# When results are stored: earlier and then later stores, buffers held one slot longer, and two sets of carries on SyncE's queue

## The chip, the core and the metric

The kernel runs on one core of a Trainium2 chip. PE is TensorE (matrix products), DVE is VectorE, ACT is ScalarE, POOL is GpSimd, and SP is SyncE, which here only issues DMA transfers. The metric is the device time of one execution in microseconds (us).

## The reference

For each of 16 batches and 256 channels, a recurrence runs over 2048 time steps. It is the weighted average of the values v with weights exp(k) that fade with time by exp(-w); `pp` only keeps the exponents from overflowing:

```python
for t in range(seq_len):
    ww = u + kk
    qq = np.maximum(pp, ww)
    e1, e2 = np.exp(pp - qq), np.exp(ww - qq)
    output[b, t, :] = (e1 * aa + e2 * vv) / (e1 * bb + e2 + 1e-08)
    ww = pp - w + kk
    qq = np.maximum(ww, kk)
    e1, e2 = np.exp(ww - qq), np.exp(kk - qq)
    aa = e1 * aa + e2 * vv
    bb = e1 * bb + e2
    pp = qq
```

Numerator and denominator are the same sum with v and without it. k and v are 33.6 MB each, the output 33.6 MB, all float32.

## The kernel before

**Tiles.** Time is cut into 16 stages of 128 steps (numbered c), the batches into 4 groups of 4. A tile n = 4c + p is stage c of group p: 128 steps on the partitions, 4 batches x 256 channels along the free side, 0.5 MB. There are 64 tiles. Each needs a load of k, a load of v and a store, each a single DMA of 0.5 MB issued by SP.

**A tile's way.** DVE rounds k into `km` (L193) and casts v to bf16 (L227), PE forms the exponents (`logs`, L203 and L209), ACT takes their exponentials (`exps`, L222), DVE multiplies these by v (`times_v`, L233). Ten slots later (LAG = 10) PE sums the denominator with a triangular matrix (`den`, L360), ACT takes its logarithm into an output buffer (`den_log`, L365) and turns it into the reciprocal there (`den_exp`, L368), PE sums the numerator (`num`, L377), DVE multiplies both (`mult`, L381), and SP stores the buffer (`store`, L385).

**Carries.** What goes from stage to stage is computed per stage in small steps: `sums`, `copy_sums`, `turn`, `state_logs`, `state_frames`, `state_scan`, `state_offsets`, `state_weights`, `state_chain`, `turn_back`, `inject`. The last one casts the carries (L345) and writes them with four small DMAs (L350) over two rows of the exponentials of the stage's own four tiles, where `den` and `num` of these tiles read them. The first two of the four go where `den` reads. POOL issues these DMAs for stages 0 to 14, SP for stage 15. The carries of stage 14 are wanted by tiles 56 to 59, those of stage 15 by tiles 60 to 63.

**Order.** The order is written out by hand: every instruction stands in its engine's queue in the order of the program. The main loop counts slots n = 0 to 63; in slot n the exponentials of tile n are taken, q = n - 10 is the tile whose denominator is formed, qp = n - 11 the one whose product is formed. The dictionary `later` places the steps for the carries in later slots. After slot 63 a tail does the last ten tiles.

**Buffers.** 19 buffers of 0.5 MB serve loads and outputs alike. `take` hands out the one whose slot number is lowest. A loaded buffer is free again in the slot in which it is cast. An output buffer is free STORED slots after the slot of its store (L386). `loads` (L79) moves a buffer from the loads' list to the outputs' when fewer than three of these will be free; then it issues loads while they are under nine slots ahead and two buffers are free. These slot numbers decide only who gets which buffer: that the store has landed is waited for on the chip, by the logarithm that writes the buffer.

**SP's queue.** SP works in program order. A load waits for the cast that frees its buffer, a store for its product. Which stores a slot issues is said in L485:

```python
while stored < (qp - 2 - max(0, n - 20) // 12 if loaded < NP else qp):
    store(stored, n)
```

So stores are two slots late at first, three from slot 32, four from slot 44, five from slot 56, and all at once when the last load has been issued. The tail stores what is left, then tile 53 (`store(q, q + LAG)`, L533), then has the last carries issued (L539), then stores the other tiles as they come. The last tile goes out in four quarters, by SP and ACT (L558).

Of the kernel before, what the change touches and what calls it, by code (L numbers as in the profile page):

```python
# [15 lines left out]
def kernel(  # L16
# [10 lines left out]
    PE, DVE, SC, POOL, SP = nc.tensor, nc.vector, nc.scalar, nc.gpsimd, nc.sync  # L27
# [4 lines left out]
    NST = T // TC  # L32
    D = 2 * Dm
    NP = 4 * NST
    RING = 12
    BUFS, OUTS = 19, 8
    STORED = 4
    LAG = 10
    RS = 2.0 ** -20
    CAP = 54.0  # L40
# [11 lines left out]
    def rows_of(x, n):  # L52
        c, p = divmod(n, 4)
        return x[4 * p:4 * p + 4, c * TC:(c + 1) * TC, :].rearrange("n t d -> t n d")
# [4 lines left out]
    free = [(0, x) for x in bufs[OUTS:]]  # L59
    free_out = [(0, x) for x in bufs[:OUTS]]  # L60

    def take(slot, of):
        j = min(range(len(of)), key=lambda j: of[j][0])
        assert of[j][0] <= slot
        return of.pop(j)[1]

    def load_k(n, slot=0):
        kr_of[n] = take(slot, free)
        K(SP.dma_start(out=kr_of[n], in_=rows_of(k, n)))

    def load_v(n, slot=0):
        vr_of[n] = take(slot, free)
        K(SP.dma_start(out=vr_of[n], in_=rows_of(v, n)))
# [3 lines left out]
    loaded = 5  # L77

    def loads(slot):  # L79
        nonlocal loaded  # L80
        if slot + 2 >= LAG and sum(x <= slot + 2 for x, _ in free_out) < 3:
            free_out.append((slot + 2, take(slot, free)))
        while loaded < NP and loaded - slot < 9 and sum(x <= slot for x, _ in free) >= 2:
            load_v(loaded, slot)
            loaded += 1
            if loaded < NP:
                load_k(loaded, slot)
# [102 lines left out]
    def round_k(n, slot=0):  # L190
        km = consts.tile([128, 4, Dm], F32R, tag=f"km{n % 2}", name="km") if n < 2 else KM[n - 2]
        kr = kr_of.pop(n)
        K(DVE.tensor_copy(km, kr))  # L193
        free.append((slot, kr))
        KM[n] = km

    def logs(n):
        km = KM[n].rearrange("p (i n) d -> p i (n d)", i=2)

        def rows(q):  # L200
            for i in range(2):
                g = 32 * (2 * q + i)
                K(PE.matmul(half(n, q)[:, i, :], CO[g:g + 32, :],  # L203
                            WU[g:g + 32, :].unsqueeze(1).broadcast_to([32, 2, Dm]), start=True, stop=False,
                            tile_position=(g, 0), skip_group_check=True))

        def steps(q):
            for i in range(2):
                K(PE.matmul(half(n, q)[:, i, :], (NLE, NLZ)[q], km[:, i, :], start=False, stop=True,  # L209
                            skip_group_check=True))  # L210

        rows(0)
        rows(1)
        steps(0)
        steps(1)

    def exps(n):
        if n < TURNS:
            for q in range(2):
                K(SC.activation(ez(n)[:, q], half(n, q), ACT.Exp))  # L220
        else:
            K(SC.activation(ez(n)[:, 0:2], PS[:, 0:4, :].rearrange("p (q i) x -> p q i x", q=2), ACT.Exp))  # L222

    def cast_v(n, slot=0):
        vb = vbpool.tile([128, 4, Dm], BF16, tag="vb", name="vb")
        vr = vr_of.pop(n)
        K(DVE.tensor_copy(vb, vr))  # L227
        free.append((slot, vr))
        VB[n] = vb

    def times_v(n):
        vb = VB.pop(n).rearrange("p (i n) d -> p i (n d)", i=2)
        K(DVE.tensor_mul(ez(n)[:, 2:4], ez(n)[:, 0:2], vb.unsqueeze(1).broadcast_to([128, 2, 2, D])))  # L233
# [109 lines left out]
    def inject(c, queue=POOL):  # L343
        cb = small.tile([128, 128], BF16, tag="cb", name="cb")
        K(DVE.tensor_copy(cb, st.pop((c, "CT"))))  # L345
        r0 = 4 * c % RING
        for q in range(2):
            for h in range(2):
                r, x = HS * h + HS - 1, 32 * (2 * q + h)
                K(queue.dma_start(  # L350
                    out=EZR[r:r + 1, 2 * q, r0:r0 + 4, :, :].rearrange("o p i (b x) -> o (p i b) x", b=4),
                    in_=cb[x:x + 32, :]))
# [4 lines left out]
    def den(n, bank=DENB):  # L357
        for m, q in (("L", 0), ("Id", 1)):
            for i in range(2):
                K(PE.matmul(bank[:, i, :], mats[m], ez(n)[:, q, i, :], start=q == 0, stop=q == 1,  # L360
                            skip_group_check=True))
# [13 lines left out]
    def num(n, bank, i):  # L375
        for m, q in (("LN", 2), ("IdN", 3)):
            K(PE.matmul(bank, mats[m], ez(n)[:, q, i, :], start=q == 2, stop=q == 3, skip_group_check=True))  # L377

    def mult(n, bank, i):
        rd = RD[n]  # L380
        K(DVE.tensor_mul(rd[:, i, :], bank, rd[:, i, :]))  # L381

    def store(n, slot):
        rd = RD.pop(n).rearrange("p i (n d) -> p (i n) d", n=2)
        K(SP.dma_start(out=rows_of(out, n), in_=rd))  # L385
        free_out.append((slot + STORED, rd))  # L386

    later = {}
    for c in range(NST):
        s = 4 * c + 3  # L390
        plan = [(s + 1, "act" if s + 1 < LAG else "recip", copy_sums), (s + 1, "pe", turn),
                (s + 2, "act", state_logs), (s + 2, "mid", state_frames), (s + 2, "scan", state_scan), (s + 2, "scan", state_offsets),
                (s + 3, "recip", state_weights), (s + 3, "chain", state_chain),
                (s + 4, "nums", turn_back), (s + 4, "mid", inject), (s + 4, "mid", state_next)]
        if c == 0:
            plan = [(s + 1, "act", copy_sums), (s + 1, "pe", turn), (s + 1, "pe", state_logs),
                    (s + 1, "round", state_frames), (s + 1, "round", state_scan), (s + 1, "round", state_offsets),
                    (s + 2, "act", state_weights), (s + 2, "round", state_chain),
                    (s + 3, "pe", turn_back), (s + 3, "round", inject), (s + 3, "round", state_next)]
        if c == 1:  # L400
            plan = [(s + 1, "act", copy_sums), (s + 1, "pe", turn), (s + 2, "act", state_logs),
                    (s + 2, "round", state_frames), (s + 2, "round", state_scan), (s + 2, "round", state_offsets),
                    (s + 3, "recip", state_weights), (s + 3, "early", state_chain)] + plan[8:]
        if c == NST - 1:
            plan = []
        for slot, where, f in plan:
            later.setdefault((slot, where), []).append((f, c))

    def small_work(n, where):
        for f, c in later.pop((n, where), []):  # L410
            f(c)
# [35 lines left out]
    stored = 0  # L447

    def inverses(n):
        q, qp = n - LAG, n - LAG - 1  # L450
        if qp >= 0:
            num(qp, NUMB, 1)

        sums(n - 1)
        if n + 1 < NP:
            recip(q, lambda: small_work(n, "recip"))

    for n in range(LAG, NP):

        q, qp = n - LAG, n - LAG - 1  # L460
        if qp >= 0:
            num(qp, NUMB, 0)
        den(q)
        small_work(n, "nums")
        exps(n)
        small_work(n, "act")
        if qp >= 0:
            mult(qp, NUMB, 0)
        small_work(n, "mid")
        if n == LAG:  # L470

            inverses(n)
            small_work(n, "early")
        if n + 2 < NP:
            round_k(n + 2, n)

        if n % 4 in (3, 0):
            cast_v(n, n)
        if n + 1 == NP:
            times_v(n)  # L480
        elif n % 4 < 2:
            cast_v(n + 1, n)
        loads(n)

        while stored < (qp - 2 - max(0, n - 20) // 12 if loaded < NP else qp):  # L485
            store(stored, n)
            stored += 1
        if n > LAG:
            inverses(n)
        if qp >= 0:  # L490
            mult(qp, NUMB, 1)
        small_work(n, "scan")
        if n + 1 < NP:
            times_v(n)
            small_work(n, "chain")
            logs(n + 1)
        small_work(n, "pe")
# [4 lines left out]
    q, c = NP - LAG - 1, NST - 1  # L502
# [4 lines left out]
    def outputs(n):  # L507
        for i in range(2):
            mult(n, nbank(n, i), i)
        store(n, n + LAG)  # L510
# [19 lines left out]
    state_offsets(c)  # L530
    state_weights(c)
    mult(q, nbank(q, 1), 1)
    store(q, q + LAG)  # L533
    state_chain(c)
    den(q + 3, dbank(q + 3))
    for i in range(2):
        tile_num(q + 1, i)
    turn_back(c)
    inject(c, SP)  # L539
    outputs(q + 1)  # L540
    for n in range(q + 2, NP):
        if n + 1 < NP:
# [8 lines left out]
    n, p = NP - 1, (NP - 1) % 4  # L551
# [38 lines left out]
```

## Time and profile before

| | |
|---|---|
| median of 3 runs | 286.34 us (285.8 to 286.8) |
| profiled execution | 285.23 us, its span 283.5 us |
| DVE busy | 261.1 us (92%) |
| PE busy | 256.2 us (90%) |
| ACT busy | 253.6 us (89%) |
| POOL busy | 106.0 us (37%) |
| moved by DMA | 101.54 MB, mean 358 GB/s |
| TensorE clock granted | 0.994 |

The span runs from the first to the last instruction of the profiled execution; 1.7 us of its time lie around it. Issuing a DMA doesn't count as busy. In lines of a timeline the columns are start (us), duration (us), engine, line and operation, written and read tiles, count, and in brackets the engine's idle time before it with what ended it. A busy share is an average over the whole span; a wait counts where something stands behind it.

### The profile page before, as it was taken

The page shows a single profiled execution, that of the slowest core. Times are in us where ns is not written, and L with a number is a line of the kernel's source. Part 1 is how long each engine was busy: PE and PEld are TensorE (multiplying, and loading weights), DVE is VectorE, ACT ScalarE, POOL GpSimd, SP SyncE. Part 2 cuts the span into 40 slices and gives each one's busy share as a digit, 9 for nine tenths or more (in the row PEclk, how much of TensorE's full clock was granted, in tenths as well). Part 3 has the DMA queues.
Part 4 walks back from the last instruction along what each step waited for, and adds up shares of the span by engine and source line. Part 5 has one row for each costly group of instructions (what it writes and reads, how often), then busy time and mean ns, then how long its engine had stood idle before and what let it go on. Part 6 is the DMA issues. An engine that isn't in the chain of part 4 may idle for free.

```text
span 283.5 us, 5049 instructions
## 1 busy us (share of the span) xinstructions
PE 256.2 (90%) x1662; PEld 119.5 (42%) x1694; DVE 261.1 (92%) x465; ACT 253.6 (89%) x252; POOL 106.0 (37%) x206
## 2 busy tenths in 40 slices
PE   6997896999999999999999999899999999997990
PEld 2444442544454444544454444444444344433430
DVE  4699989999999999999999999999999999987863
ACT  2576678999999999999999999899999999997991
POOL 7000424263445444253445445143546546242000
PEclk9999999999999999999999999999999999999997
DMA  6999999999999999999999999999999999999597
GB/s 225 349 348 350 348 331 350 333 348 352 384 375 382 384 381 385 383 382 382 384 377 384 375 384 377 378 376 369 382 379 384 383 384 378 380 384 334 167 340 252
DMA packets 103586, 101.54 MB, mean 358 GB/s; under 512 B 4284, under 2 KB 103560, under 8 KB 103560
## 3 DMA queue, kind: packets, MB, share of 16 engines
q1 hardware_dynamic: 101336, 100.45, 103.9%
q0 software_dynamic: 1920, 0.50, 0.8%
q8 instruction: 13, 0.21, 0.3%
q10 hardware_dynamic: 304, 0.27, 0.3%
q14 instruction: 13, 0.11, 0.1%
HBM read 67.12 MB, written 33.55 MB: 355 GB/s over the span
## 4 chain that ended last, share of the span: by engine, by line
DVE 35%; PE 27%; DMA 16%; ACT 9%; issue 9%; DVEq 1%; POOL 0%; ACTq 0%; POOLq 0%
DVE EZR L233 14%; DVE buf L381 11%; PE PS L377 9%; PE PS L209 9%; DMA buf<-in_k_dram 7%; DMA out_dram<-buf 6%; PE PS L257 3%; PE PS L203 3%; ACT EZR L222 3%; ACT buf L365 3%; DVE vb L227 3%; DVE km L193 3%; PE PS L360 2%; ACT buf L368 2%; DMA EZR<-cb 2%
## 5 line engine op out<-in xcount | busy, mean ns | idle before, releaser
L222 ACT ACTIVATE EZR<-PS 128x2048 bf16<-128x2048 f32 x54 | 101.2, 1874 | 3.3 <-PE PS L209 2.6
L381 DVE TENSOR_TENSOR buf<-PS,buf 128x512 f32<-128x512 f32 x128 | 87.6, 692 | 6.3 <-ACT buf L368 4.2
L233 DVE TENSOR_TENSOR EZR<-EZR,vb 128x2048 bf16<-128x2048 bf16 x64 | 78.3, 1224 | 3.1 <-ACT EZR L220 2.5
L365 ACT ACTIVATE buf<-PS 128x1024 f32<-128x1024 f32 x64 | 65.8, 1028 | 3.4 <-DMA out_dram<-buf 1.6
L368 ACT ACTIVATE buf<-buf 128x1024 f32<-128x1024 f32 (+1 forms) x65 | 67.9, 1049 | 0.9
L377 PE MATMUL PS<-EZR,LN 128*128 128x512 bf16 x128 | 48.8, 381 | 10.3 <-DVE buf L381 6.7
L350 POOL DMA_DIRECT2D EZR<-cb x60 | 36.7, 617 | 52.0 <-DVE cb L345 44.6
L209 PE MATMUL PS<-km,NLE 128*128 128x512 f32 x128 | 47.6, 454 | 1.8 <-DVE km L193 1.8
L193 DVE CAST km<-buf 128x1024 fp32r<-128x1024 f32 x64 | 44.2, 691 | 1.3 <-DMA buf<-in_k_dram 1.2
L227 DVE CAST vb<-buf 128x1024 bf16<-128x1024 f32 x64 | 43.3, 695 | 0.0
L377 PE MATMUL PS<-EZR,IdN 128*128 128x512 bf16 x112 | 42.4, 378 | 0.0
L209 PE MATMUL PS<-km,NLZ 128*128 128x512 f32 x128 | 41.0, 403 | 0.0
L360 PE MATMUL PS<-EZR,L 128*128 128x512 bf16 x128 | 38.1, 379 | 1.6 <-DMA EZR<-cb 1.6
L360 PE MATMUL PS<-EZR,Id 128*128 128x512 bf16 x115 | 35.3, 379 | 0.0
L288 POOL TENSOR_TENSOR F<-LL,LL 128x32 f32<-128x32 f32 x13 | 8.5, 654 | 63.6 <-ACT LL L279 63.6
L203 PE MATMUL PS<-WU,CO 32*128 32x512 bf16 x256 | 26.9, 393 | 2.7 <-DVE WU L421 1.6
L257 PE MATMUL PS<-EZR,OH 128*32 128x256 bf16 x512 | 26.2, 277 | 2.9 <-ACT LL L279 0.7
L209 PEld LDWEIGHTS PS<-km,NLZ 128*128 128x128 f32 x128 | 24.6, 192 | 5.7
L220 ACT ACTIVATE EZR<-PS 128x1024 bf16<-128x1024 f32 x20 | 19.4, 1020 | 8.4 <-PE PS L209 8.4
L209 PEld LDWEIGHTS PS<-km,NLE 128*128 128x128 f32 x128 | 19.4, 191 | 17.0 <-issue 12.9
L377 PEld LDWEIGHTS <-IdN 128*128 128x128 bf16 x128 | 12.5, 97 | 23.0 <-issue 20.8
L377 PEld LDWEIGHTS <-LN 128*128 128x128 bf16 x128 | 12.8, 100 | 18.3 <-issue 11.3
(71 smaller groups left out, 202.8 us busy)
## 6 DMA issues: line engine op xcount, KB each, us to landing
buf<-in_k_dram SPq DMA_DIRECT2D x64, 512.0 KB, 8.2
buf<-in_v_dram SPq DMA_DIRECT2D x64, 512.0 KB, 8.1
out_dram<-buf SPq DMA_DIRECT2D x63, 512.0 KB, 8.0
EZR<-cb POOLq DMA_DIRECT2D x60, 8.0 KB, 5.3
out_dram<-buf SPq DMA_DIRECT2D x2, 128.0 KB, 3.3
out_dram<-buf ACTq DMA_DIRECT2D x2, 128.0 KB, 3.2
EZR<-cb SPq DMA_DIRECT2D x4, 8.0 KB, 1.9
wuf<-in_w_dram ACTq DMA_DIRECT2D x1, 8.0 KB
```

The lines of the kernel that those rows point to most:

```text
L193: K(DVE.tensor_copy(km, kr))
L203: K(PE.matmul(half(n, q)[:, i, :], CO[g:g + 32, :], WU[g:g + 32, :].unsqueeze(1).broadcast_to([32, 2, Dm]), start=True, stop=False, tile_p ...
L209: K(PE.matmul(half(n, q)[:, i, :], (NLE, NLZ)[q], km[:, i, :], start=False, stop=True, skip_group_check=True))
L222: K(SC.activation(ez(n)[:, 0:2], PS[:, 0:4, :].rearrange("p (q i) x -> p q i x", q=2), ACT.Exp))
L227: K(DVE.tensor_copy(vb, vr))
L233: K(DVE.tensor_mul(ez(n)[:, 2:4], ez(n)[:, 0:2], vb.unsqueeze(1).broadcast_to([128, 2, 2, D])))
L350: K(queue.dma_start(out=EZR[r:r + 1, 2 * q, r0:r0 + 4, :, :].rearrange("o p i (b x) -> o (p i b) x", b=4), in_=cb[x:x + 32, :]))
L360: K(PE.matmul(bank[:, i, :], mats[m], ez(n)[:, q, i, :], start=q == 0, stop=q == 1, skip_group_check=True))
L365: K(SC.activation(RD[n], bank, ACT.Ln, scale=RS))
L368: K(SC.activation(RD[n][:, i, :], RD[n][:, i, :], ACT.Exp, scale=-1.0))
L377: K(PE.matmul(bank, mats[m], ez(n)[:, q, i, :], start=q == 2, stop=q == 3, skip_group_check=True))
L381: K(DVE.tensor_mul(rd[:, i, :], bank, rd[:, i, :]))
```

## The change

- An output buffer may be handed out again five slots after its store's slot, not four.
- Loads are issued under seven slots ahead, not nine.
- Stores: in the main loop a tile is stored in the slot after its product at first (none late); one slot late from slot 22, two from 27, three from 32, four from 37; three in slot 60, two in 61, one in 62 and 63. The store of everything at once after the last load is gone.
- The carries of stage 14 are issued by SP, as those of stage 15 were.
- In the tail the store of tile 53 comes after the carries of stage 15 on SP's queue, not before them.

```diff
-    STORED = 4
+    STORED = 5
...
-        while loaded < NP and loaded - slot < 9 and sum(x <= slot for x, _ in free) >= 2:
+        while loaded < NP and loaded - slot < 7 and sum(x <= slot for x, _ in free) >= 2:
...
-                (s + 4, "nums", turn_back), (s + 4, "mid", inject), (s + 4, "mid", state_next)]
+                (s + 4, "nums", turn_back), (s + 4, "mid", inject if c < NST - 2 else lambda c: inject(c, SP)),
+                (s + 4, "mid", state_next)]
...
-        while stored < (qp - 2 - max(0, n - 20) // 12 if loaded < NP else qp):
+        while stored < qp - (min(4, max(0, n - 17) // 5) if n < NP - 4 else max(1, NP - 1 - n)):
             store(stored, n)
             stored += 1
...
     mult(q, nbank(q, 1), 1)
-    store(q, q + LAG)
     state_chain(c)
...
     inject(c, SP)
+    store(q, q + LAG)
     outputs(q + 1)
```

## The prediction

> **What bounds the kernel now.** I read the table of busy shares first: DVE 92%, PE 90%, ACT 89%, none of them alone the bound. So next the slices in time, then the waits.
>
> ```profile
> DMA  6999999999999999999999999999999999999597
> GB/s 225 349 348 350 348 331 350 333 348 352 384 375 382 384 381 385 383 382 382 384 377 384 375 384 377 378 376 369 382 379 384 383 384 378 380 384 334 167 340 252
> ```
>
> The DMA engines are full from the first slice to the 36th, at about 350 GB/s while there are only loads and 380 once stores are mixed in. The hole is in slice 38 (262 to 269 us). Compute and transfers are matched: the exponentials of slots 16 and 32 start at 64.11 and 127.69 us, so an undisturbed slot takes 63.58/16 = 3.974 us, and its three transfers of 0.524 MB at 380 GB/s take 3 x 1.38 = 4.14 us. Transfers fall behind compute, and whatever depends on a store's landing becomes late. The timeline of ACT shows it:
>
> ```profile
> 142.29 1.03 ACT L365 ACTIVATE buf<-PS 128x1024 f32<-128x1024 f32 x1 [0.65 <-DMA out_dram<-buf]
> ...
> 178.50 1.03 ACT L365 ACTIVATE buf<-PS 128x1024 f32<-128x1024 f32 x1 [0.70 <-DMA out_dram<-buf]
> ...
> 198.69 1.02 ACT L365 ACTIVATE buf<-PS 128x1024 f32<-128x1024 f32 x1 [0.22 <-DMA out_dram<-buf]
> ```
>
> The logarithm waits for the store that still holds its output buffer: 1.57 us in three places. What that costs: slot 60 starts at 240.03, and 44 slots of 3.974 after 64.11 would be 238.95. So 1.08 us are lost.
>
> The end, in the timelines of PE, ACT and SP:
>
> ```profile
> 260.10 0.59 PE L360 MATMUL PS<-EZR,L 128*128 128x512 bf16 x2 [1.55 <-DMA EZR<-cb]
> 261.16 1.02 ACT L365 ACTIVATE buf<-PS 128x1024 f32<-128x1024 f32 x1 [1.48 <-PE PS L360]
> 240.20 20.12 SPq L385 DMA_DIRECT2D out_dram<-buf  x12
> 262.57 2.52 SPq L350 DMA_DIRECT2D EZR<-cb  x4
> 265.19 12.80 SPq L385 DMA_DIRECT2D out_dram<-buf  x9
> 278.18 1.40 SPq L558 DMA_DIRECT2D out_dram<-buf  x2
> ```
>
> PE and ACT stand until the carries of stage 14 (issued by POOL at 253.95) land at 259.97. From 261.16 on ACT takes about 1.86 us per tile up to 277.2. SP sends stores 42 to 53, then must wait for the last carries, sends those until 265.1, and only then stores 54 to 62 and the four quarter pieces of 63. And these stores are near a bound of their own. Busy time by stretches:
>
> ```profile
> 247.00:258.00 11.00, 10.58 (x70) 4.63 (x71) 9.67 (x19) 10.35 (x11) 5.26 (x12) 1.00 1.08 380
> 266.00:281.00 15.00, 10.46 (x46) 4.31 (x45) 9.55 (x16) 11.27 (x13) 0.00 (x0) 0.97 0.99 334
> ```
>
> (The last three columns are clock, DMA share and GB/s.) Both stretches hold stores alone, the first in a deep queue. In the second they land 1.54 us apart (268.33, 269.86, 271.42 ... 280.68), and the last piece at 282.18, then 1.3 us to the end of the span.
>
> **What the skill says.** "DMA: Bandwidth & Descriptors", section "Issuing engines are not separate DMA queues": transfers issued from any engine run on the same 16 DMA engines and interleave. The trace agrees: POOL's 8 KB carries need 5.3 us (median) amid the big ones, SyncE's 1.9 us in the hole. Its section "Queues, rings and completion order" says that a DMA engine takes turns between queue rows but works one row in order. So a carry on SyncE's queue stands behind every store issued before it. The trace agrees in one place: store 53 landed at 264.26, the first carry of stage 15 behind it at 264.47. "HBM Reference", "Specifications", gives 358 GB/s as a core's share and more for a core alone; the measured 380 is above that share, so I use the measured rates.
>
> **The change part by part.** I numbered SyncE's transfers in both kernels. The same number means about the same time, since the queue is full.
>
> *Stores one to two slots sooner.* Store 0 moves from place 44 (issued at 63.23) to place 40 (about 56.6). Stores up to 13 are 3 to 7 us sooner, later ones within 3 us of before. Some 6.2 us of pure loads become mixed traffic: 6.2 x (1 - 346/380) = 0.55 us gained on the transfer clock, call it 0.5; bounds 0 and 0.6. All of them up to 49 are ready at least 6 us before their place, so none blocks the queue.
>
> *Loads seven slots ahead instead of nine.* Loads move back at most three places (3 us, around tile 20). The least slack between landing and use was 1.5 us (k of tile 62). At the old clock it becomes 0.6 (k of 60 and 61), 1.1 (k of 56). With compute 1.05 sooner and transfers 0.5 sooner it is about 0. I price it at nothing with 0.5 us as the upper bound. Were that cover gone, DVE would stand in the cast of k, and with it the products behind it. A buffer to load into is free at least 0.4 us before its place.
>
> *Buffers reused five slots after a store.* For every logarithm I took the landing (issue + 8.1) of the store that its buffer waits for. Before, the slack was 0.1 to 0.6 us in slots 28 to 35 and 0.0 to 0.4 at 40, 41, 44 and 45; after it is at least 3.0. The 1.57 us of waits go, and with them 1.08 us at slot 60: -1.05, bounds -0.5 (loads late instead) and -1.1.
>
> *Carries of stage 14 from SyncE.* Store 49 keeps its place (250.07, now about 249.6). Stores 48 and 50 landed at 256.96 and 259.74, so 49 at about 258.35, and now at 257.85. The carries are cast at 253.66 - 1.05 = 252.6, and the four issues of 0.63 us last until 255.2. They land behind store 49, the first two (which the denominator needs) by 258.2 instead of 259.97. PE would be ready at 258.55 - 1.05 = 257.5, so 0.7 us of the 1.55 stays. The denominators then start 1.85 sooner; the turn-back of stage 15 needs its CB (260.96 - 1.05 = 259.9), and comes at about 259.95 instead of 261.83; so cast and last carries go -1.85 too (SP at 260.7). Blocked behind the carries on SyncE: stores 50 to 52, sent at 255.3 to 256.1 and landed at about 262.3. Their buffers are wanted near 270. POOL loses four issues (2.05 us), hidden: it was idle for 3.57 us before them.
>
> *Store 53 behind the last carries.* SP is free of these at 260.7 + 2.6 = 263.3 instead of 265.19. But eleven stores' worth are then left instead of ten. In the old sum: 265.19 + 3.14 (issue to landing of 54) + 9 x 1.54 = 282.19, which is the trace. In the new: 263.3 + 3.14 + 10 x r. With r = 1.54 it is 281.85 (-0.3); with r = 1.38, as in a deep queue, 280.2 (-1.9), about where compute ends it anyway (278.78 - 1.85 + 3.4 = 280.3). Stores stand in the queue about one deeper than before, so I take r = 1.47: 281.15, that is -1.0.
>
> **Sum.** Span 283.5 - 1.0 = 282.5, so the profiled execution 285.23 - 1.0 = 284.2. The median of the runs is 286.34, 1.1 above that execution; on it -1.0 gives 285.3. A change under 0.3% (0.86 us) can hardly be told from none here.
>
> **Rivals.**
> *The end runs into stores at the slow rate* (r = 1.54). For it: 334 GB/s held for 15 us. Against: three or four were in flight around 255 to 258 at 380. Then -0.35: 286.0, no difference.
> *Compute sets the end.* The eleven stores keep up, and all of the -1.85 arrives: 284.5. For it: stores at 380 GB/s just before; against: the measured tail.
> *Slower: store 53 counts in full.* The place is the last carries on SyncE. If stage 15's carries don't come sooner (loads eat the middle's gain, and the carries of stage 14 land at 260 as before behind the stores), the eleventh store adds 1.54 us to a chain that starts where it did: 286.34 + 1.2 to 1.5 = 287.7. It decides if these carries come less than 0.7 us sooner. Against it: store 49 was issued 3.9 us before the POOL carries of stage 14, so its queue is half empty by then.
> *The change doesn't do what it says:* waits for stores stay. The slack of 3 us speaks against it; I give it no chance of its own.
>
> **How the numbers follow.** Forecast (285.3) 0.40; compute sets the end (284.5) 0.15; slow rate (286.0) 0.28; slower (287.7) 0.17. The forecast's own spread, 284.8 to 285.9, passes the bound for no change (285.48), so a fifth of it goes to "same", and some of the slow-rate and slower cases cross as well: faster 0.52, same 0.33, slower 0.15. The range leaves out a little of the fastest and the worst of the slower case: 284.0 to 287.3. The likeliest one's own range is 284.8 to 285.9.
>
> **What would show it.** In the profile after: no wait of L365 for a store in the middle; slot 60 at 239.0 within 0.4; a wait of PE for carries of 0.5 to 1.0 us near 258; the last carries on SyncE near 260.7; then ten full stores landing 1.4 to 1.54 apart. I am wrong in the middle if DVE waits for k near slots 54 to 61, and wrong at the end if PE still waits over 1.3 us for the carries, or if the stores after the last carries land further apart.

## The result, and the profile after

The changed kernel is not faster. Over 20 runs beside 20 of the kernel before, its median is 286.54 us against 285.5. The ratio estimated from all these runs is 1.0029, with a 95% interval of [1.0016, 1.0043], so it is about 0.83 us slower (by the medians alone 1.04) where 1.0 us less was forecast. (The 286.34 of the three runs shown first lies high among the 20.) Its profiled execution took 285.63 us, span 283.9; before 285.23 and 283.5. This execution lies 0.9 us under the median of its kernel, so the two profiles differ by only 0.4.

The first 64 us, where the pipeline fills, vary from execution to execution by up to 4 us. In two kernels below that are alike up to slot 50, slot 16 began at 67.81 and at 63.89 us. The clock granted to TensorE (the third number from the end) differed in the fill, here from 40 to 50 us:

```profile
40.00:50.00 10.00, 7.44 (x47) 3.05 (x46) 8.87 (x21) 7.08 (x7) 2.51 (x6) 0.82 1.10 346
40.00:50.00 10.00, 7.96 (x57) 3.48 (x60) 9.76 (x24) 8.49 (x9) 3.15 (x7) 1.00 1.10 349
```

In all 18 profiles of this case slot 16 begins by 64.81 us where the clock from 40 to 64 us is 1.00, and at 65.33 or later where it is 0.93 or 0.86; the clock from 10 to 20 us doesn't sort them. So I cut every span at fixed instructions and compare from slot 16 on:

| us, from the profiles | before | after | predicted | measured |
|---|---|---|---|---|
| start to exponentials of slot 16 (L222) | 64.11 | 63.95 | | -0.16 |
| slots 16 to 63 | 187.78 | 187.58 | -1.05 | -0.20 |
| slot 63 to cast of stage 15's carries (L345) | 10.37 | 9.59 | -0.80 | -0.78 |
| this cast to the last product (L381) | 16.50 | 16.50 | 0 | 0 |
| last product to the end of the span | 4.77 | 6.31 | +0.85 | +1.54 |
| span | 283.5 | 283.9 | -1.0 | +0.4 |

(The predicted +0.85 is the rest of the forecast: the cast 1.85 sooner, the end only 1.0.) One term came as computed, one gain of 0.85 didn't come, and the tail (below always the time from the last product to the end of the span) cost 0.7 more.

The page's slices of the changed kernel, 7.1 us each:

```profile
DMA  6999999999999999999999999999999999998697
GB/s 199 358 349 349 348 330 349 332 359 378 385 380 382 383 376 385 381 380 383 380 366 385 374 379 384 380 377 380 377 382 378 378 384 380 377 372 268 217 339 263
```

Mixed traffic (375 GB/s and more) now begins one slice sooner, as foreseen. But the hole near the end has become two slices, 268 and 217 GB/s (256 to 270 us), where there was one of 167 after one of 334.

What DVE and ACT waited for in the changed kernel (engine, line, what ended the wait: us in all, times, longest):

```profile
DVE km L193 <- DMA buf<-in_k_dram: 1.9, 3, 0.9
...
DVE vb L227 <- DMA buf<-in_v_dram: 1.1, 1, 1.1
...
ACT buf L365 <- PE PS L360: 0.6, 1, 0.6
```

No logarithm waits for a store any more; before, that was 1.57 us in three places. The wait for v and two of the three for k lie in the fill, where the kernel before waits for k as well. The third wait for k is new, and is the one that counts. The timeline of DVE shows it in slot 58, at the cast of k of tile 60, and then the cast of stage 15's carries, which came at 262.25 before:

```profile
232.95 0.76 DVE L193 CAST km<-buf 128x1024 fp32r<-128x1024 f32 x1 [0.76 <-DMA buf<-in_k_dram]
...
261.12 0.29 DVE L345 CAST cb<-PS 128x128 bf16<-128x128 f32 x1 [0.49 <-PE PS L339]
```

Up to there the slots had gained: against before, slot 36 starts 0.84 us sooner, slot 45 1.49, slot 54 1.31. Slot 60 is only 0.54 ahead, slot 63 0.35. The gain of the middle was made, and then lost at its end.

How much the middle (slots 16 to 63) loses depends on when slot 16 begins. Undisturbed, its 47 slots of 3.974 us take 186.78. Eight profiles below share the changed kernel's main loop up to slot 62: begun at 63.71, 63.95 and 64.53, the middle took 187.88, 187.58 and 187.31; begun at 65.34 or later (five profiles), 186.69 to 186.83, with no wait for k. Three profiles share the main loop of the kernel before: begun at 64.08, 64.11 and 64.52, it took 188.09, 187.78 and 187.11. So the loss of 1.08 us from which the forecast started is that of one execution, and the change's loss of 0.80 is one of early starts. What the kernel before loses after a late start is not on record.

Carries of stage 14 land at 258.01 and 258.20 (before 259.97). The weight load for their denominator, from the timeline of PE's weight loads, waited 0.58 us for them, where it had waited 2.0 us before:

```profile
258.31 0.13 PEld L360 LDWEIGHTS <-L 128*128 128x128 bf16 x2 [0.58 <-DMA EZR<-cb]
```

And SP's queue, from 240 us on:

```profile
240.42 1.18 SPq L73 DMA_DIRECT2D buf<-in_v_dram  x1
241.99 9.48 SPq L385 DMA_DIRECT2D out_dram<-buf  x7
253.36 2.79 SPq L350 DMA_DIRECT2D EZR<-cb  x4
256.23 2.18 SPq L385 DMA_DIRECT2D out_dram<-buf  x3
261.49 2.69 SPq L350 DMA_DIRECT2D EZR<-cb  x4
264.27 12.59 SPq L385 DMA_DIRECT2D out_dram<-buf  x10
277.05 2.44 SPq L559 DMA_DIRECT2D out_dram<-buf  x2
```

SP is free of the last carries (below: its release) at 264.27, 0.92 us sooner than the 265.19 of before, and ten full stores follow instead of nine. Stretches of the changed kernel (start:end, length, busy time of PE, PEld, DVE, ACT and POOL, then clock, DMA share, GB/s):

```profile
247.00:255.00 8.00, 7.64 (x52) 3.15 (x52) 7.14 (x13) 7.90 (x8) 3.17 (x7) 1.00 1.08 381
255.00:258.00 3.00, 2.91 (x21) 1.28 (x20) 2.42 (x7) 2.35 (x4) 0.00 (x0) 1.00 0.69 231
258.00:262.00 4.00, 3.43 (x19) 1.44 (x19) 3.37 (x14) 3.35 (x6) 0.00 (x0) 1.00 1.01 336
262.00:266.00 4.00, 3.95 (x19) 1.84 (x19) 3.16 (x7) 4.00 (x5) 0.00 (x0) 1.00 0.24 71
267.00:282.00 15.00, 8.32 (x36) 3.36 (x35) 7.85 (x13) 9.14 (x11) 0.00 (x0) 0.93 1.03 341
```

The DMA engines run short twice while SP stands before carries, at 255 to 258 and at 262 to 266, and afterwards stores land 1.545 us apart. From the release, 3.11 us to the first landing and ten more places of 1.545 (the four quarter pieces count as one) give the last landing: 264.27 + 3.11 + 10 x 1.545 = 282.83. The same sum for before is 265.19 + 3.14 + 9 x 1.54 = 282.19. Store 53, sent at 259.95 before, had landed at 264.26, in time that is now a hole.

### The profile page after: what moved, and what is told of

Read it like the earlier page. It is cut to its first block, busy times and chain, and to the rows that moved or that the text cites. A ratio compares the mean times of both kernels' runs of the same rounds, so it can differ in the third digit from the quotient of the medians.

```text
span 283.9 us, 5053 instructions
## 1 busy us (share of the span) xinstructions
PE 256.4 (90%) x1662; PEld 119.5 (42%) x1694; DVE 260.8 (92%) x465; ACT 253.7 (89%) x252; POOL 105.1 (37%) x202
## 4 chain that ended last, share of the span: by engine, by line
DVE 34%; PE 23%; DMA 17%; ACT 12%; issue 10%; DVEq 1%; POOL 0%; POOLq 0%; ACTq 0%
DVE EZR L233 13%; DVE buf L381 11%; PE PS L377 8%; PE PS L209 8%; DMA buf<-in_k_dram 7%; DMA out_dram<-buf 5%; ACT buf L365 5%; DMA buf<-in_v_dram 4%; ACT buf L368 3%; DVE km L193 3%; PE PS L257 3%; PE PS L203 3%; DVE vb L227 2%; ACT EZR L222 2%; DMA wuf<-in_u_dram 2%
## 5 line engine op out<-in xcount | busy, mean ns | idle before, releaser
L222 ACT ACTIVATE EZR<-PS 128x2048 bf16<-128x2048 f32 x54 | 101.3, 1876 | 4.8 <-PE PS L209 3.6
L381 DVE TENSOR_TENSOR buf<-PS,buf 128x512 f32<-128x512 f32 x128 | 86.7, 685 | 5.5 <-ACT buf L368 3.6
L365 ACT ACTIVATE buf<-PS 128x1024 f32<-128x1024 f32 x64 | 65.9, 1029 | 0.7 <-PE PS L360 0.6
L350 POOL DMA_DIRECT2D EZR<-cb x56 | 34.3, 618 | 48.3 <-DVE cb L345 41.2
L288 POOL TENSOR_TENSOR F<-LL,LL 128x32 f32<-128x32 f32 x13 | 9.4, 723 | 62.1 <-ACT LL L279 62.1
```

Of the source, the lines that this page charges most:

```text
L365: K(SC.activation(RD[n], bank, ACT.Ln, scale=RS))
```

## The experiments

The theory after the result: (A) the tail is a chain of SP's release plus 1.54 us per store left, so store 53 costs a full 1.54; (B) the middle's gain is eaten because loads of the last tiles come one place later and transfers, not compute, set slots 60 to 63. The rival to A: the depth of the queue, or the carries of stage 14 on SP, slow the tail. The rival to B: the stores' places, rather than the loads. Ratios are to the kernel before. Parts of a kernel's time are read from one profiled execution each.

### Store 53: back to its place, and alone behind the carries

In the changed kernel:

```diff
     mult(q, nbank(q, 1), 1)
+    store(q, q + LAG)
     state_chain(c)
...
     inject(c, SP)
-    store(q, q + LAG)
```

> The changed kernel with one thing put back: the store of tile 53 ahead of the carries of stage 15 on SyncE's queue. Theory A (the end is a chain of stores 1.54 us apart that starts when SyncE is done with these carries, so the moved store adds one whole store): ten stores' worth instead of eleven after the carries, last landing 1.5 us sooner than in the changed kernel, span about 282.4, ratio to the kernel before 0.9975. Theory B (the loss comes from loads that are late near slot 60): no change against the changed kernel, ratio 1.003.

And in the kernel before, the reverse edit alone:

> The kernel before with one part of the change alone: the store of tile 53 behind the carries of stage 15 on SyncE's queue. Theory A: these carries are issued at 262.6 as before, eleven stores' worth follow, the last lands 1.5 us later, span 285.0, ratio 1.005. Theory B: no difference, ratio 1.000.

Measured: the first 286.0 us, 1.0007 [0.9988, 1.0026]; the second 287.61 us, 1.0069 [1.0046, 1.0092]. SP's queue of the first, then of the second:

```profile
262.46 3.00 SPq L350 DMA_DIRECT2D EZR<-cb  x4
265.56 12.31 SPq L385 DMA_DIRECT2D out_dram<-buf  x9
```

```profile
262.29 2.51 SPq L350 DMA_DIRECT2D EZR<-cb  x4
264.89 12.76 SPq L385 DMA_DIRECT2D out_dram<-buf  x10
```

In the second kernel the release is only 0.30 us sooner than before: store 53 no longer stands ahead of the carries, but the carries themselves are hardly earlier. Its last landing is 283.45 = 264.89 + 3.1 + 10 x 1.546. Its tail takes 6.36 us, against 4.77. With store 53 back in its place (first kernel) the tail is 5.05, against 6.31. So by the profiles one store moved behind the carries costs 1.3 to 1.6 us of tail, with or without the rest of the change. The timed runs show it clearly in the second kernel (1.97 us, from six runs). In the first, putting the store back gained only 0.22%, 0.63 us, on the changed kernel, and the two intervals meet; theory A had expected 0.9975.

A second store moved, as well (the changed kernel with store 52 behind the carries too, one execution):

```diff
-    for n in range(stored, q):
+    for n in range(stored, q - 1):
...
+    store(q - 1, q + LAG)
     store(q, q + LAG)
```

> The changed kernel with store 52 too behind the carries of stage 15. Theory A: twelve stores' worth instead of eleven, last landing 1.54 us later than in the changed kernel when counted from SyncE's release: release + 3.1 + 11 x 1.54; span about 285.4. Rival: span 283.9.

```profile
256.62 1.08 SPq L385 DMA_DIRECT2D out_dram<-buf  x2
261.96 2.42 SPq L350 DMA_DIRECT2D EZR<-cb  x4
264.43 13.33 SPq L385 DMA_DIRECT2D out_dram<-buf  x11
```

From SP's queue: 264.43 + 3.15 + 11 x 1.545 = 284.6, which is where its last piece landed; span 285.7. The sum holds for nine, ten and eleven stores. So A holds for the tail; that a store behind the carries also costs time as a whole is shown by the second kernel above.

### Does a deep queue make the stores faster?

My forecast had taken 1.47 us per store, because stores before the hole land 1.38 us apart. Two edits were to hold the stores 53 to 62 of the changed kernel back and release them at once. The first put their calls, in order, behind the loop of the tail:

```diff
     inject(c, SP)
-    store(q, q + LAG)
...
+    for n in range(q, NP - 1):
+        store(n, n + LAG)
```

(the stores inside the loop go as well).

> The changed kernel with stores 53 to 62 all held until the last product of tile 62, then issued one after another: slow on purpose, to see the rate of stores in a deep queue with compute over. If depth makes stores fast (as the prediction took it): they land 1.38 us apart. If the end of the kernel has the slow rate whatever the depth: 1.54 us apart. The last landing is at about 293.2 or 294.8.

It was no test: SP's own sequence is the same as in the changed kernel, and a store waits only for its own product. One execution gave 286.02, span 284.3, with the wait for k of tile 60 again (0.87 us): a repeat of the changed kernel. The second edit has SP send store 62 first, so that all the others stand ready behind it:

```diff
+    for n in [NP - 2] + list(range(q, NP - 2)):
+        store(n, n + LAG)
```

> The changed kernel with the store of tile 62 moved ahead of stores 53 to 61 on SyncE's queue: SyncE waits for tile 62's product (near 276.5), then has ten stores to issue at once, a deep queue from dry DMA engines. The run with stores held in the program's order had not held them, since SyncE's own order was the same. If depth makes stores fast: they land 1.38 us apart, last landing near 293. If stores that start from dry engines go at the slow rate whatever the depth: 1.54 us apart, last landing near 295.

One execution took 299.59 us, as it must with the stores held until the end. Its stretches and SP's queue:

```profile
247.00:255.00 8.00, 7.72 (x53) 3.42 (x53) 7.25 (x15) 7.97 (x9) 4.09 (x9) 1.00 1.09 385
280.00:296.00 16.00, 0.00 (x0) 0.00 (x0) 0.00 (x0) 0.00 (x0) 0.00 (x0) 0.53 1.04 340
```

```profile
278.33 11.95 SPq L385 DMA_DIRECT2D out_dram<-buf  x10
290.38 2.61 SPq L559 DMA_DIRECT2D out_dram<-buf  x2
```

With ten stores ready at once, and no compute beside them, they land at 286.82, 288.36, 289.91, 291.45 and 293.02: 1.54 us apart, 340 GB/s. Each takes 6.4 to 7.1 us from issue to landing, so four or five are in flight at a time, where two or three are in the tail of the kernel before. This depth doesn't make them faster, and neither compute nor carries are what makes them slow. In the kernel before, 255 to 258 us ran at 370 GB/s with as many in flight; in the execution here, 247 to 255 ran at 385. These fast stores follow directly on mixed traffic, the slow ones on a stretch in which the DMA engines stood, also between the two holes of the changed kernel (336 GB/s from 258 to 262). Why this is so stays open.

### The carries of stage 14: back to POOL

```diff
-                (s + 4, "nums", turn_back), (s + 4, "mid", inject if c < NST - 2 else lambda c: inject(c, SP)),
+                (s + 4, "nums", turn_back), (s + 4, "mid", inject),
```

> The changed kernel with the carries of stage 14 issued by POOL again. Theory A: the carries land near 259 instead of 258.2, PE and with it the last carries are 0.4 to 0.9 us later, and so is the end: ratio 1.0045 to 1.006. Rival (SyncE, blocked by the carries of stage 14 for 3 us, holds stores 50 to 52 back and the DMA engines run dry near 256, and this is what the end pays): 0.5 to 1 us sooner, ratio 1.000.

Measured 287.59 us, 1.0067 [1.0041, 1.0092], from six runs; SP free at 264.86 instead of 264.27, slot 63 to cast 10.04 instead of 9.59, tail 6.37. So in the changed kernel this part is a gain, 1.0029 against 1.0067 (the intervals just touch). It shortens the way to the last carries as forecast, and is not what costs; the rival, that the hole at 255 to 258 us slows the end, had expected 1.000.

### The last carries away from SP

If SP's standing before the last carries is what makes the tail, it should go when another queue sends these. In the changed kernel, with store 53 back in its old place:

```diff
-    inject(c, SP)
-    store(q, q + LAG)
+    inject(c)
```

> The changed kernel with the store of tile 53 ahead again and the carries of stage 15 issued by POOL, so that no store stands behind them on SyncE. Theory A (the end is SyncE's release from these carries, then 3.1 us, then 1.54 us a store): the chain no longer starts at the carries; compute sets the end, last product near 277.6, last landing near 281.2, ratio 0.996 to 0.998. If POOL's carries land after the denominator of tile 60 wants them (about 266.5), the end moves back by that much, to 1.000 or above. Rival (the DMA engines' total work bounds the end, wherever the stores stand): ratio 1.001 as with the store put back alone.

Measured 284.89 us, 0.9967 [0.9949, 0.9985]. The tail is 4.43 us, which is what compute needs without a queue of stores before it. Against the changed kernel that is -1.88 in the tail, and the two ratios differ by 0.62%, 1.77 us. Both edits have a part in this: with store 53 back alone it was 1.0007 and a tail of 5.05. With only one pair of carries on POOL and the other on SP:

```diff
-                K(queue.dma_start(
+                K((queue if q == 0 or c < NST - 1 else POOL).dma_start(
```

> The changed kernel with the store of tile 53 ahead again, and of the four carries of stage 15 two on SyncE and two on POOL. Theory A: SyncE is released 1.3 us sooner than with four, the stores that follow end 1.3 us sooner or when compute lets them: last landing 281 to 281.5, ratio 0.996 to 0.998. Rival: 1.001.

285.03 us, 0.9978 [0.9966, 0.9990], tail 4.66: SP was free at 263.89 with nine stores left. No better than all on POOL. And the kernel before with only its last carries on POOL:

> The kernel before with the carries of stage 15 issued by POOL, nothing else. In the kernel before the last store lands 19.9 us after these carries are cast, and compute alone would need 19.8. So theory A gives ratio 1.000, at best 0.999: the gain of the version with POOL doesn't come from POOL but from carries of stage 14 that are sooner, as long as no store waits behind those of stage 15. Rival (SyncE's stop of 2.6 us for the carries costs the end by itself): ratio 0.996.

285.34 us, 0.9988 [0.9977, 0.9999]. There the tail had only 4.77 - 4.43 = 0.34 us to give. The 0.12% are 0.34 us as well, but with an interval of 0.03 to 0.66, and its own profile shows a tail of 4.55; the close agreement is luck, the small size is not. So in the kernel before, the tail was all but bound by compute; the change made it bound by stores.

### The middle: later stores at its end

Stores one slot later from slot 50 give their places to the last loads:

```diff
-        while stored < qp - (min(4, max(0, n - 17) // 5) if n < NP - 4 else max(1, NP - 1 - n)):
+        while stored < qp - (min(4 + (n >= 50), max(0, n - 17) // 5) if n < NP - 4 else max(1, NP - 1 - n)):
```

> The changed kernel with stores five slots late from slot 50 on, so that the loads of tiles 55 to 61 stand in their old places on SyncE's queue (one sooner than in the changed kernel). Theory B: the wait of DVE for the k of tile 60 (0.76 us) goes, and with it 0.75 us at the last carries and at the end, ratio 1.000. Theory A together with B expects the same; theory A alone (the transfers bound the end whatever the engines do) expects no difference to the changed kernel, ratio 1.003.

Measured 286.28 us, 1.0033 [1.0019, 1.0046], not the 1.000 that theory B expected. The profile, begun at 64.44, has the middle at 186.79, so nothing is lost, and no wait for k near its end; the cast of the last carries came at 260.85, 0.27 sooner than in the changed kernel. But SP was free only at 264.45, because its four carries took 3.14 us to issue instead of 2.69, and the tail is 6.75. The gain of the middle went into the tail, which is bound by stores. With the last carries on POOL as well:

> The changed kernel with the store of tile 53 ahead again, the carries of stage 15 on POOL, and stores five late from slot 50 on (loads of tiles 55 to 61 in their old places). If the late load of tile 60 costs 0.3 to 1 us once the stores no longer bound the end: ratio 0.994 to 0.996. Rival (nothing left there): 0.997 as without it.

284.8 us, 0.9968 [0.9952, 0.9983]: the same as without the later stores (0.9967). In this execution slot 16 began early (63.89), and of the 3.3 us that DVE waited for k, 1.8 us in four places lie in the middle, which took 188.81. So after an early start moving the stores doesn't free the loads: it only moves the place of the wait. That suggests that the transfers as a whole are late (theory C). To test it, four transfers are left out, so that tiles 20 to 23 of the output are not written:

```diff
-        K(SP.dma_start(out=rows_of(out, n), in_=rd))
+        if not 20 <= n < 24:
+            K(SP.dma_start(out=rows_of(out, n), in_=rd))
```

> The changed kernel without the stores of tiles 20 to 23 (left out, their part of the output is not written), so four transfers less stand ahead of all later loads. Theory C (with the waits for stores gone, slot 63 is bound by the transfers' own clock, k arriving late): the later loads are 5.5 us sooner, no wait for k after slot 40, slots 16 to 63 take 186.8 us instead of 187.6; the end gains at most that, ratio 0.999 to 1.001. Rival (the engines' own work or something else bounds the middle): slots 16 to 63 as in the changed kernel, 187.6, waits as before.

285.88 us, 1.0013 [0.9997, 1.0028]. Slot 63 began at 250.96, against 251.53 in the changed kernel and 251.88 before, with nearly the same start (64.02), and the middle took 186.95. One wait for k of 0.18 us is left in it. So with an early start the last slots are set by transfers: 4 x 1.38 us less of these gave 0.6 of the 0.8 us that compute had to gain. The timed runs agree in direction, but their interval meets that of the changed kernel (1.0029 [1.0016, 1.0043]).

### The parts of the middle: fifth slot and stores' places

The kernel before with `STORED = 5` alone:

> The kernel before with output buffers reused five slots after the store, nothing else. Theory of the prediction (1.08 us of waits for stores go): ratio 0.997. Rival (what is taken from the stores' waits comes back as waits for loads, of which several then stand one place later): ratio 1.000.

286.7 us, 1.0047 [1.0028, 1.0065], from six runs: slower than either theory had expected. Its waits for k:

```profile
DVE km L193 <- DMA buf<-in_k_dram: 2.4, 5, 1.0
```

Four of the five places lie in the fill; in the middle there is one wait of 0.47 us, at 234.8. This profile doesn't show the cost: slot 16 begins at 65.97, and from there on every part takes no longer than before (middle 187.31, slot 63 to cast 10.11, tail 4.75). The changed kernel with `STORED = 4`:

> The changed kernel with output buffers reused four slots after a store, as before. The loads of tiles 55 to 61 then stand in their old places on SyncE, so it was the fifth slot that moved them. Theory C: no wait for k near slot 60, but stores can be waited for again (slack 3.0 less 3.97 in slots 28 to 31, about 1 us); the two about cancel, ratio 1.001 to 1.004. If the fifth slot was worth the 1.08 us of the prediction: 1.0065.

286.29 us, 1.0019 [1.0005, 1.0033], as theory C expected. The order of loads of tiles 55 to 61 is then that of the kernel before, and still no logarithm waits for a store. The kernel before with only the new condition for stores (L485):

> The kernel before with the stores' new places in the main loop, nothing else. Theory C (transfers bound the middle; moving stores among loads moves no bytes): ratio 0.999 to 1.002. Prediction's theory (0.5 us of transfer clock and fewer waits for stores): 0.997.

285.07 us, 0.9970 [0.9953, 0.9986]: the number of the prediction's theory, and under the 0.999 that theory C gave as its least. No logarithm waits for a store here either. So by the timed runs the stores' places are the part that pays, and they remove the waits without the fifth slot, which alone costs 0.47%. The profile doesn't show where the 0.30% comes from: its middle, begun at 64.81, took 187.27, within the 187.11 to 188.09 of the old places. In the changed kernel the cost of the fifth slot (1.0029 against 1.0019) is within the intervals. Last, stores' places and carries of stage 14 as changed, buffers held four slots, store 53 first and the last carries on POOL:

```diff
-    STORED = 5
+    STORED = 4
...
+    store(q, q + LAG)
     state_chain(c)
...
-    inject(c, SP)
-    store(q, q + LAG)
+    inject(c)
```

> The version with the store of tile 53 ahead and the carries of stage 15 on POOL, with buffers reused four slots after a store. If the fifth slot only pushes loads back: 0.994 to 0.996, better than the same with five (0.9967). If it takes the waits for stores away for good: 0.999.

284.31 us, 0.9955 [0.9936, 0.9974], faster than the kernel before and the changed one. Its interval overlaps those of the version with five slots (0.9967) and of the stores' places alone (0.9970), so that it is the fastest of these isn't shown. Its queues of SP and of POOL:

```profile
255.29 2.52 SPq L350 DMA_DIRECT2D EZR<-cb  x4
257.90 20.88 SPq L385 DMA_DIRECT2D out_dram<-buf  x13
278.97 1.35 SPq L559 DMA_DIRECT2D out_dram<-buf  x2
```

```profile
263.89 2.05 POOL L350 DMA_DIRECT2D EZR<-cb  x4 [8.99 <-ACT buf L368]
```

After 257.90 SP stands before no carries; stores leave as their products come, and the tail is 4.43 us, as with five slots.

## Why the prediction was wrong

Two steps failed: the loads, priced at nothing, and the sum for the tail, in which SP's release and the time per store were mis-sized. Only the second shows in every profile of a kernel with store 53 behind SP's last carries: its tail is 6.04 to 6.75 us (longer only in the two kernels that hold more stores back).

**The stores' places (right in the waits, wrong in the clock).** The waits of L365 went, as said. The 0.5 us on the transfer clock (the times at which the same places in SP's queue are issued) hardly came: transfer 60 of SP's queue was issued 0.3 us sooner than before, transfer 120 0.4 later, and transfer 171 at 240.42 against 240.20. (This one is the load of v of tile 63 in the changed kernel; before, this load stood one place sooner, at 238.68.) My reading, not shown, is that a gain is lost again wherever SP waits for a buffer or a product; what counts is where the clock stands at the last loads.

**Loads (the step that failed in the middle).** I priced them at nothing, with slack "about 0" and 0.5 us as the upper bound. Measured in the profile: 0.85 of the 1.05 us didn't come, nearly all of it by one wait of DVE for k, 0.76 us in slot 58, where I had said I would be wrong. The size of the gain was not safe either: it was read from one execution that lost 1.08 us at slot 60, and two more of the same main loop lost 0.33 and 1.31 by slot 63. The reason I gave for later loads was also wrong: the limit of seven instead of nine slots ahead is not felt, since with nine the changed kernel's program puts the same transfers in the same order; free buffers bind first. The fifth slot takes a buffer from the loads, and so moves some of those of tiles 51 to 61 one place back (k of 60 is issued at 224.81, before 223.54). Freeing them again (`STORED = 4`) brought little, though, so the deeper reason is the one that four stores less supports: from slot 36 on compute was up to 1.5 us ahead of before on a transfer clock no faster than before, and had to wait for it somewhere. My reading is that the waits for stores that I counted as gained were in part the same debt, paid at another engine. This holds for early starts; after a late one no k was late in the changed kernel's middle. And it leaves open how the stores' places alone gained 0.30%.

**Carries of stage 14 (right).** Landing at 258.2 as computed, the logarithm behind it waiting 0.61 us instead of 1.48 (PE was to keep 0.7), slot 63 to cast -0.78 for -0.80. In absolute time the cast came 1.13 sooner instead of 1.85, because the middle brought only 0.20.

**Store 53 and the tail (the step that failed at the end).** The sum was right in form: release, 3.1, ten stores. Two terms were mis-sized. The release came at 264.27 instead of 263.3: 0.72 because the cast came later than forecast, the rest mostly from one issue of a carry that took 0.81 us. And r was 1.545, not 1.47, which over ten stores is 0.75 us. I had taken a value between two measured rates, on the thought that the deeper queue would be faster; it is 1.54 with ten stores ready, too. Even with the release at 263.3, r = 1.545 would have left only 0.3 us of the forecast 1.0. The Trainium skill ("DMA: Bandwidth & Descriptors", "Queues, rings and completion order") has the work of one queue row consumed in order. The trace agrees: the ten stores behind the carries landed one after the other, from 267.38 to 281.35. So store 53 behind the carries took a whole place of this row; ahead of them it had landed at 264.26, while SP stood. (The landing that I had named for this order shows nothing: that carry took 1.90 us, as carries with nothing ahead of them do, 1.81 to 1.83. Those of stage 14 show it: issued from 253.36 to 255.60 behind store 49, all four landed within 258.01 to 258.56.) What store 53 made way for, the landing of the carries, bound nothing: from their cast to the last product it is 16.50 us with the store ahead of them and without.

**What reaches the timed runs.** The carries of stage 14 brought -0.78 us and the tail cost +1.54, in sum +0.76, close to the +0.83 of the runs. So the middle probably brought little in them; no profile of the kernel before with a late start shows it.

**The rivals.** The slower one, "store 53 counts in full", is what happened in mechanism and in sign, at 0.8 us instead of 1.2 to 1.5. Its own condition (last carries less than 0.7 us sooner) was not met: SP was free 0.92 sooner. With r = 1.545 the stores of the tail break even only where SP is free 1.54 sooner. The rate was that of the slow-rate rival, whose -0.35 failed for lack of the middle's gain. "Compute sets the end" holds only where SP doesn't stop.

**The sum by parts.** Alone in the kernel before: stores' places -0.30%, fifth slot +0.47%, store 53 behind the carries +0.69%; carries of stage 14 on SP, from the changed kernel, -0.38%. Together +0.48%, measured +0.29%; each term has an interval of about 0.2% to either side, so the sum agrees within the noise. Open are also why the fifth slot alone costs a full 0.47%, where its one profile is after slot 16 no longer than that of before, and why a carry's issue takes up to 1.25 us (in the kernel with later stores) where 0.54 is usual.

## What to carry to other kernels

Where an engine issues transfers in order and must stand before an urgent small one, and a full chain of transfers follows, send everything that is ready ahead of it: the hole is free room, and a transfer put behind it costs its full time in the chain. Whether the small one is better off in another queue depends on the traffic: for stage 15, with few stores in flight, POOL's queue was better (0.9967 against 1.0007), for stage 14, amid a full queue, SP's own (1.0029 against 1.0067). Before counting a removed wait as gained time, ask which clock was late, and look at more than one execution: if transfers bound the stretch, the wait can come back at another engine.

## What was not expected of the hardware

Half-megabyte stores alone ran at 334 to 341 GB/s (1.54 us each) after the DMA engines had stood, and at 380 to 385 GB/s directly after a stretch mixed with loads; how many were in flight doesn't explain it. Four carries of 8 KB hold SP for 2.4 to 3.2 us. POOL sends the same four in 2.05 us in the tail.
